# Scan of a bidirectional RWKV layer: TensorE in a written order, products on 64-wide tiles

## The chip, the cores and the metric

The kernel runs on one core of one Trainium2 chip. The metric is device time in microseconds of one execution, measured on the chip. Five engines work side by side, each with its own queue of instructions: TensorE (PE, matrix products into PSUM), VectorE (DVE), ScalarE (ACT), GpSimd (POOL) and SyncE (SP). SP, ACT and POOL also issue DMA transfers between the main memory and SBUF. An engine executes its queue in order and waits where an instruction needs something that another engine or a DMA has not delivered.

## The reference, cut to what matters

One layer works on 128 context tokens and 2048 latent tokens. A combined projection gives r, k, v, gates and a short convolution; eight heads of 64 channels then run a delta-rule recurrence over time, in both directions:

```python
def step(S, inp):
    r_t, w_t, k_t, v_t, kk_t, a_t = inp
    s_kk = jnp.einsum('bdhij,bdhj->bdhi', S, kk_t)
    S = (S * w_t[..., None, :] - s_kk[..., :, None] * (kk_t * a_t)[..., None, :]
         + v_t[..., :, None] * k_t[..., None, :])
    return S, jnp.einsum('bdhij,bdhj->bdhi', S, r_t)
```

Outputs of both directions are added, normalised per head, gated, joined with the convolution's channels and sent through an output projection with a residual and a final norm. Outputs are the new context, the new latent tokens and the final context states. All is float32.

## The kernel before, in words

The program has three parts. `phase1` computes projections, gates and the operands of the recurrence, and stores them in DRAM (`scr_ops`, `scr_vt` and others). `phase2` does the recurrence. `phase3` does the output projection; part of it (`ahead`) is woven into the last stages of the recurrence.

The recurrence is cut into chunks of 64 tokens. Within a chunk the state update is written as products of matrices, with the inverse of a unit triangular matrix of 64 x 64, and only the state passes from chunk to chunk. A **stage** (`NST = 17`) has two groups, one for each direction, with eight chunk units each; a unit has two heads (a head pair `p`). Stage 15 is the context, the others take four blocks of 512 tokens for each of four head pairs. The work of a stage s goes through these parts, in the names of the code and of the profile:

- `partL`: loads the operands of a group into `rr` (issued on SP).
- `partM`: products F and GA (psF, psG, masked by DVE into F and GA), the transposes psQ (copied by ACT into Q), and `blocks`, which puts the two 32 x 32 triangular blocks of GA together (dg, on ACT and DVE) and writes them to DRAM (`scr_at`, issued on ACT).
- `partI`: loads these blocks as `ab` (issued on SP) and inverts all of a stage at once on POOL, by some 50 element-wise instructions of one chain; POOL then writes the result zt to DRAM (`scr_zt`).
- `partW`: loads the stacks `stl` and `str`, the values `sv` and the inverse `zc` (SP), and copies GA and Q into the lower half of the stacks (DVE, ACT).
- `partU`: completes the inverse of 64 x 64 from its blocks of 32: zr is a transposed zc (DVE), psU and psW are products on tiles of 32 x 32, and ACT copies the pieces into `zb`. In the program before, `zb` is a tile of 128 x 128 per unit with zeros outside its two diagonal blocks.
- `partB`: product X (psX, of zb and F), copied with a minus by ACT into the stacks; then product E (psE, of the two stacks), masked by DVE into E.
- `partS`: the scan itself. In eight steps it multiplies E by sv (psS); DVE scales the upper half into the next step's sv (line 998), the lower half goes to the output y.
- `finish`: norm and gate of a finished y, a transpose on TensorE (psT), and the store to `scr_mixT`.

While stage s scans, `partB` runs for stage s + 1, and `partM` and `partI` for stage s + 3 (`LA = 3`, three slots of F, GA and Q). Python generators interleave these parts in the order in which the instructions are written; `ORDER` and the tuple of counts in `main` say which part advances after which scan step. That order is a preference only: a planner reorders each engine's instructions by its own estimate of when operands are ready, and so sets the queues of all engines, SP's included. In the loop, `partI` of stage s + 3 is written at the end of stage s:

```python
            run(m)
            if s + LA + 1 < NST:
                sts[s + LA + 1] = partL(s + LA + 1)
            if s + LA < NST:
                partI(s + LA, sts[s + LA])
```

The load of zc for stage s + 1 is written in the first piece of `partW` (line 891), at the start of stage s; the load of ab is line 847, POOL's first use of it line 856, POOL's output line 868.

PSUM has three pools here: `pm` (two banks: F, GA, Q), `p2` (two banks: X, E, U, W, the transposes of finish) and `pS` (four banks: the scan).

Of the kernel before, what the change touches and what calls it, by code (L numbers as in the profile page):

```python
# [617 lines left out]
NST = 17  # L618
MORD = ("F", "GD", "", "Q")
ON_DVE = "g"  # L620
LA = 3


ORDER_END = ('LbbbL', 'UU', 'U', '', 'BBB', '', '', '', '')
ORDER = ('LbbbL', '', 'U', 'U', 'U', '', 'BBB', '', '')


def phase2(K):
# [42 lines left out]
    def setup_rest():  # L671
# [17 lines left out]
        lt = ring(O.l1, 2, [128, 2, 2, 4, 128], "stl", lambda t_: presetS(vl(t_)))  # L689
        rt = ring(O.l1, 2, [128, 2, 2, 2, 4, 64], "str", presetS)  # L690
        B.lt, B.rt = lambda: vl(lt()), rt
        B.bu = O.l1.tile([128, 16, 32], F32, name="bu")
        B.zb = O.l1.tile([128, 2, 8, 128], F32, name="zb")
        zero(B.zb)
# [30 lines left out]
    def vl(t_):  # L725
        return t_[:].rearrange("p f h u (b t) -> p b f h u t", b=2)

    def presetS(t_):
        for f in range(2):
            for hd in range(2):  # L730
                V.tensor_copy(t_[0:64, 0, f, hd], B.I2[0:64].unsqueeze(1).broadcast_to((64, 4, 64)))
# [34 lines left out]
    def load_stk(t_, g, k, us):  # L766

        units = g.units[us]
        p, c0 = units[0]
        src = S[f"ops{g.d}"][k]  # L770
        n = 4 if p == units[-1][0] else 2
        for i in range(4 // n):
            dst = t_[0:64, 1, us.start // 4, :, n * i:n * (i + 1)]
            x = src[(p + i) * 128:(p + i + 1) * 128, c0 * 64:(c0 + n) * 64]
            if t_ is g.rt:
                D(dst.rearrange("c h u t -> c h (u t)"), x.rearrange("(h c) t -> c h t", h=2))
            else:
                for hd in range(2):
                    D(dst[:, hd], x[hd * 64:hd * 64 + 64].rearrange("c (u t) -> c u t", t=64))
# [6 lines left out]
    def partL(s):  # L786
        st = Ctx()
        st.g = []
        for gi, (d, units, blk) in enumerate(stages[s]):
# [12 lines left out]
        return st  # L802

    def partM(s, st):

        at = S["at"][s]
        for gi, g in enumerate(st.g):
# [3 lines left out]
            g.Q = q[:].rearrange("p (k u) t -> p k (u t)", u=2)  # L811
            def transposes():
                pq = O.pm.tile([128, 4, 128], F32, tag="m", name=f"psQ{s}_{gi}")
                for k in range(4):
                    T.transpose(pq[:, k, :], rr[:, 4, 2 * k:2 * k + 2, :].rearrange("p u t -> p (u t)"), B.idt[:])
                copy("q", g.Q, pq[:])
# [527 lines left out]
```

## Time and profile before

| | us |
|---|---|
| median of 3 runs | 1832.66 (1829.14 to 1839.34) |
| the profiled execution | 1837.07 |
| its span, first to last instruction | 1835.3 |
| scan products (psS), first to last start | 1044.6 to 1669.3 |

In the profile, line numbers are those of the kernel before. PE stands for products on TensorE, PEld for its weight loads, which overlap them. A float32 product is two instructions of each kind. SPq, ACTq and POOLq mark the issue of a DMA. A row of a group of instructions has busy time, mean duration in ns, and the idle time of the engine ahead of it with what ended it. A row of a stretch has its bounds, its length, each engine's busy time with a count of instructions, the granted TensorE clock, the mean busy share of the 16 DMA engines, and GB/s.

### The profile page before, as it was taken

How to read it: one execution, taken by the hardware profiler on the slowest of the kernel's cores; microseconds unless marked ns; L12 is line 12 of the kernel's file. 1: busy time of each engine (PE TensorE's matmuls, PEld its weight loads, DVE VectorE, ACT ScalarE, POOL GpSimd, SP SyncE). 2: the span in 40 equal slices, each digit the busy share in tenths (PEclk: the TensorE clock that was granted, in tenths of full speed). 3: DMA queues.
4: the chain of work that ended last, by engine and by line, in shares of the span. 5: the costliest groups of instructions: out<-in, count | busy, mean ns of one | idle time of the engine just before them, and what ended most of it. 6: DMA issues, size and time to landing. Idle time of an engine off the chain costs nothing. (4 is left out here: it accounts for less than half of the span.)

```text
span 1835.3 us, 35161 instructions
## 1 busy us (share of the span) xinstructions
PE 1685.3 (92%) x13488; PEld 1553.3 (85%) x13488; DVE 1151.2 (63%) x2205; ACT 748.4 (41%) x1471; POOL 595.1 (32%) x1087
## 2 busy tenths in 40 slices
PE   5999899999898999999999798899899899799998
PEld 2998899898888999899899687788798798687886
DVE  5999887446777363588543555576577466656433
ACT  4565545124444131465211353354354336442222
POOL 0132200002221000223055166567657765523221
PEclk9999999999999999999999798799899779899999
DMA  8787787557887353677863665577567655546442
GB/s 350 223 242 240 226 266 266 202 182 161 190 192 189 126 189 132 178 207 201 308 216 120 141 162 116 135 179 176 129 171 165 162 138 143 148 133 210 147 151 98
DMA packets 315384, 335.29 MB, mean 183 GB/s; under 512 B 166920, under 2 KB 263560, under 8 KB 301136
## 3 DMA queue, kind: packets, MB, share of 16 engines
q1 hardware_dynamic: 242912, 323.99, 59.7%
q10 hardware_dynamic: 70944, 4.60, 2.9%
q0 software_dynamic: 1360, 4.46, 0.6%
q8 instruction: 106, 1.74, 0.4%
q14 instruction: 62, 0.51, 0.1%
HBM read 221.16 MB, written 111.82 MB: 181 GB/s over the span
## 5 line engine op out<-in xcount | busy, mean ns | idle before, releaser
L867 POOL TENSOR_TENSOR zt<-zt,ztmp 128x30 f32<-128x30 f32 (+7 forms) x510 | 200.9, 394 | 39.6
L945 PE MATMUL psE<-str,stl 128*128 128x128 f32 x1088 | 158.9, 294 | 22.4 <-DVE E L946 21.4
L945 PEld LDWEIGHTS psE<-str,stl 128*128 128x128 f32 x1088 | 138.9, 201 | 33.4 <-DVE E L946 22.0
L985 PE MATMUL psS<-sv,E 128*128 128x64 f32 x1088 | 159.0, 283 | 8.3 <-DVE sv L998 8.3
L985 PEld LDWEIGHTS psS<-sv,E 128*128 128x128 f32 x1088 | 148.3, 204 | 16.1 <-DVE sv L998 9.8
L864 POOL TENSOR_TENSOR ztmp<-ab,zt 128x60 f32<-128x60 f32 (+7 forms) x255 | 132.2, 518 | 19.9
L946 DVE TENSOR_TENSOR E<-psE,msk 128x512 f32<-128x512 f32 x136 | 93.4, 689 | 59.3 <-PE psE L945 57.6
L314 POOL TENSOR_TENSOR shk<-rawl 128x384 f32<-128x384 f32 (+1 forms) x24 | 20.9, 870 | 274.8 <-ACT rawl L310 274.7
L998 DVE TENSOR_TENSOR sv<-psS,pc 64x128 f32<-64x128 f32 x254 | 67.3, 277 | 60.7 <-PE psS L985 58.6
L934 PE MATMUL psX<-F,zb 128*128 128x128 f32 x544 | 86.2, 307 | 7.6 <-DVE E L946 3.7
L1280 POOL TENSOR_TENSOR z<-z,x 128x512 f32<-128x512 f32 x32 | 43.6, 1366 | 129.1 <-DVE z L1276 107.3
L158 PE MATMUL mmv<-h,w 128*128 128x384 f32 (+1 forms) x192 | 68.0, 354 | 18.7 <-ACT q1r L312 10.6
L934 PEld LDWEIGHTS psX<-F,zb 128*128 128x128 f32 x544 | 74.8, 213 | 12.2 <-ACT zb L713 5.4
L824 PE MATMUL psF<-rr 64*64 64x128 f32 x1088 | 75.1, 300 | 10.3 <-DMA rr<-scr_ops 5.6
L824 PE MATMUL psG<-rr 64*64 64x128 f32 x1088 | 72.0, 295 | 6.9 <-DVE F L826 6.9
L824 PEld LDWEIGHTS psF<-rr 64*64 64x64 f32 x1088 | 52.1, 145 | 21.3 <-issue 4.4
L824 PEld LDWEIGHTS psG<-rr 64*64 64x64 f32 x1088 | 55.7, 143 | 13.7 <-DVE F L826 7.4
L158 PE MATMUL mmg<-h,w 128*128 128x384 f32 (+1 forms) x192 | 63.4, 330 | 3.8 <-ACT ta L374 1.8
L160 PE MATMUL mmv<-h,w 128*128 128x384 f32 (+1 forms) x192 | 66.4, 346 | 0.1
L159 PE MATMUL mmv<-h,w 128*128 128x384 f32 (+1 forms) x192 | 66.2, 345 | 0.0
L195 POOL TENSOR_TENSOR hsls<-sq,hshs 128x384 fp32r<-128x384 f32 (+1 forms) x24 | 30.0, 1252 | 107.9 <-ACT hshs L194 31.7
L158 PE MATMUL mmc<-h,w 128*128 128x384 f32 (+1 forms) x192 | 64.2, 335 | 0.5 <-DMA w<-scr_wsp 0.5
(306 smaller groups left out, 5115.4 us busy)
## 6 DMA issues: line engine op xcount, KB each, us to landing
w<-scr_wsp SPq DMA_DIRECT2D x68, 1024.0 KB, 7.2
scr_wsp<-w SPq DMA_DIRECT2D x34, 1024.0 KB, 5.8
rr<-scr_ops SPq DMA_DIRECT2D x64, 512.0 KB, 5.3
scr_ops<-sp SPq DMA_DIRECT2D x160, 192.0 KB, 4.4
wr<-in_win SPq DMA_DIRECT2D x34, 512.0 KB, 7.4
ab<-scr_at SPq DMA_DIRECT2D x34, 256.0 KB, 4.5
x<-in_x SPq DMA_DIRECT2D x17, 512.0 KB, 3.8
wadas<-in_wada SPq DMA_DIRECT2D x8, 1024.0 KB, 15.0
```

Source lines behind the costliest of these rows:

```text
L158: T.matmul(ps[:, :n], w[:, 0, k], hh[:, 0, k, :n], start=k == 0, stop=False)
L159: T.matmul(ps[:, :n], w[:, 0, k], hh[:, 1, k, :n], start=False, stop=False)
L160: T.matmul(ps[:, :n], w[:, 1, k], hh[:, 0, k, :n], start=False, stop=k == 7)
L824: T.matmul(ps[h][er, a, :].rearrange("p (a b) -> p a b", b=64), w[hr_, u, :], x[hr_, :, u, :], start=True, stop=True)
L864: G.tensor_tensor(tv, ab[:, j:j + 2, j + 2:32].unsqueeze(1).broadcast_to((128, kn, 2, n)), zt[:, :kn, j:j + 2].unsqueeze(3).broadcast_to(( ...
L867: G.tensor_tensor(zt[:, :kn, j + 2:32], zt[:, :kn, j + 2:32], tv[:, :, r], ALU.subtract)
L934: T.matmul(px[:, hd * 2 + a, :], B.zb[:, gi, v, :], g.F[:, v, :], start=True, stop=True)
L945: T.matmul(pe[:, i, hd, :].rearrange("p (b t) -> p b t", b=2), g.lt[:, :, us.start // 4, hd, k + i].rearrange("p b t -> p (b t)"), g.rt[:, ...
L946: V.tensor_tensor(g.E[n][:, k:k + 2].rearrange("p a b c -> p (a b) c"), pe[:].rearrange("p a b c -> p (a b) c"), B.msk[:, ME[g.d]].unsquee ...
L985: T.matmul(sp[gi][:, q, hd, :], g.E[n][:, k, hd, :], sv[:, u, hd, :], start=True, stop=True)
L998: r = V.tensor_tensor(dst, sp[gi][0:64, q], B.pc[0:64, d, 2 * p:2 * p + 2, c:c + 1].broadcast_to((64, 2, 64)), ALU.mult)
L1280: (V if last else G).tensor_tensor(z[:, cs], z[:, cs], xt[:, cs], ALU.add)
```

## The change

TensorE no longer follows the planner in the scan: from stage 0 to the end of stage 13 its instructions run in the order written (`tc.manual_schedule(engines={PE})`). The other engines and SP's queue are still the planner's. `ORDER` has eight slots, one after each scan step; a letter advances one part: b and B the products X and E (b of the stage that is scanning, B of the next), W and U `partW` and `partU` of the next stage, M `partM` of stage s + 3, I `partI` of stage s + 3, l and r the loads of a group of stage s + 4, z the load of the inverse of stage s + 2.

Products E and S, and the transposes of finish, are split into two halves of 64 output rows; X, before one product on a block-diagonal 128 x 128 tile, becomes two of 64 x 64; the transposes Q become products with an identity, on 64 x 64 tiles. X of the second group goes to the pool `pm`. Both stacks have one layout now and are loaded whole, in one transfer per group and operand; the copies from GA and Q are half as many and twice as long. The inverse is loaded straight into `zb`, in eight transfers, two `zb` taking turns; `zc` and the copies from it are gone.

```diff
-MORD = ("F", "GD", "", "Q")
+MORD = ("F", "GD", "Q")
-ORDER_END = ('LbbbL', 'UU', 'U', '', 'BBB', '', '', '', '')
-ORDER = ('LbbbL', '', 'U', 'U', 'U', '', 'BBB', '', '')
+ORDER = ("bM", "bMW", "UUMW", "UMWl", "MBI", "BM", "B", "Brz")
...
+            def tiles(dst, w, x):
                 for a in range(4):
                     for h, hr_ in enumerate((H0, H1)):
                         for e, er in enumerate((H0, H1)):
                             u = 2 * a + e
-                            T.matmul(ps[h][er, a, :].rearrange("p (a b) -> p a b", b=64), w[hr_, u, :], x[hr_, :, u, :], start=True, stop=True)
+                            T.matmul(dst(h, a, er), w[hr_, u, :], x(hr_, u), start=True, stop=True)
...
+            def transposes():
+                ps = banks("Q")
+                tiles(lambda h, a, er: ps[h][er, a, 0:64], rr[:, 4], lambda hr_, u: rr[hr_, 2, u, :])
+                for h in range(2):
+                    copy("q", g.Q[:, h * 4:h * 4 + 4], ps[h][:, :, 0:64])
...
+    def load_z(s, st):
+        st.zb = B.zb()
+        for h in range(2):
+            for sl in range(2):
+                for b in range(2):
+                    r = slice(sl * 64 + b * 32 + h, sl * 64 + b * 32 + 32, 2)
+                    D(st.zb[r, :, b * 32:b * 32 + 32], S["zt"][s][h][:, sl, b].rearrange("u q i -> q u i"))
...
     def partU(s, st):
-        r = V.transpose(st.zr[:].rearrange("p u i -> p (u i)"), st.zc[:].rearrange("p u i -> p (u i)"))
+        r = V.transpose(zr[:], st.zb[:, :, 0:32])
...
-        zf = B.zb[:].rearrange("p d u c -> p (d u) c")
         for r0, r1 in rows:
-            for r in (r0, r1):
-                copy("z", zf[r, :, r], st.zc[r])
-            copy("n", zf[r0, :, r1], pw[r0], True)
+            copy("n", st.zb[r0, :, 32:64], pw[r0], True)
...
     def partB(s, st):
+        for gi, g in enumerate(st.g):
+            pool, tag = (O.pm, "m") if gi and s < NST - 3 else (O.p2, "s")
+            px = [pool.tile([128, 4, 128], F32, tag=tag, name=f"psX{s}_{gi}_{e}") for e in range(2)]
+            for a in range(4):
+                for e, er in enumerate((H0, H1)):
+                    for hd, hr_ in enumerate((H0, H1)):
+                        T.matmul(px[e][hr_, a, :], st.zb[er, gi * 8 + hd * 4 + a, :], g.F[er, hd * 4 + a, :], start=True, stop=True)
+            for e in range(2):
+                for hd, hr_ in enumerate((H0, H1)):
+                    copy("x" if hd else "y", g.fs[64:128, :, hd, e::2], px[e][hr_].rearrange("p a (b t) -> p b a t", b=2), True)
+            yield
...
-                            T.matmul(pe[:, i, hd, :].rearrange("p (b t) -> p b t", b=2), g.lt[:, :, us.start // 4, hd, k + i].rearrange("p b t -> p (b t)"), g.rt[:, :, us.start // 4, hd, k + i], start=True, stop=True)
+                            for b, r in enumerate((H0, H1)):
+                                T.matmul(pe[r, i, hd, :].rearrange("p (b t) -> p b t", b=2), g.lt[:, b, hd, us.start + k + i], g.rt[:, :, hd, us.start + k + i], start=True, stop=True)
...
-                    T.matmul(sp[gi][:, q, hd, :], g.E[n][:, k, hd, :], sv[:, u, hd, :], start=True, stop=True)
+                    for r in (H0, H1):
+                        T.matmul(sp[gi][r, q, hd, :], g.E[n][:, k, hd, r], sv[:, u, hd, :], start=True, stop=True)
...
+        order = tc.manual_schedule(engines={mybir.EngineType.PE})
         for s in range(NST):
+            if s == 0:
+                order.__enter__()
+            if s == NST - 3:
+                order.__exit__(None, None, None)
...
+            for i, _ in enumerate(partS(s, st, nxt)):
                 for f in todo[:1] if s < NST - 3 else todo:
                     next(f, None)
+                next(tail, None)
+                for c in ORDER[i]:
+                    if c in gens:
+                        next(gens[c], None)
+                    elif c in "lr" and s + LA + 1 < NST:
+                        partL(s + LA + 1, ("lr".index(c),))
+                    elif c == "I" and s + LA < NST:
+                        partI(s + LA, sts[s + LA])
+                    elif c == "z" and s + 2 < NST:
+                        load_z(s + 2, sts[s + 2])
```

More of the change, by code (lines that the diff above doesn't have):

```diff
@@ L810, in partM @@
             g.F, g.GA, q = B.slots[s % LA][gi]
[L811 to L816, printed above, removed]
-            def product(dst, w, x, mask, nm):
-                ps = [O.pm.tile([128, 4, 128], F32, tag="m", name=f"ps{nm}{s}_{gi}_{h}") for h in range(2)]
+            g.Q = q[:]
+            def tiles(dst, w, x):
                 for a in range(4):
@@ L948, in partB @@
                 yield
+    ynew = {}
+    sts = {}
+    held = {}
+    pend = []
     def partS(s, st, nxt):
```

146 lines of the change are left out of this document (52 added, 94 removed).

## The prediction

> **What bounds the kernel now.** I read the page first, then stretches of the scan, then the queues between POOL and the loads.
>
> ```profile
> PE 1685.3 (92%) x13488; PEld 1553.3 (85%) x13488; DVE 1151.2 (63%) x2205; ACT 748.4 (41%) x1471; POOL 595.1 (32%) x1087
> PEclk9999999999999999999999798799899779899999
> ```
>
> By the page TensorE is the bound, with a clock that drops only in the scan (slices 23 to 36). The stretches show more. The first row counts the scan's own products (psS, 64 a stage): 896 are 14 stages in 510.90 us, 36.5 a stage.
>
> ```profile
> 1044.70:1555.60 510.90, 132.57 (x896) 0.91 0.62 149
> ```
>
> The next rows are single stretches, with PE, PEld, DVE, ACT and POOL busy, then the granted clock: a stage at full clock, one at 0.78, the last three stages, and the output projection.
>
> ```profile
> 1228.10:1259.00 30.90, 30.90 (x431) 27.82 (x430) 21.60 (x49) 18.58 (x37) 23.49 (x50) 1.00 0.70 168
> 1148.80:1195.60 46.80, 38.18 (x422) 33.67 (x422) 26.37 (x59) 17.27 (x33) 24.96 (x56) 0.78 0.62 151
> 1555.60:1669.40 113.80, 96.90 (x842) 86.97 (x841) 66.97 (x139) 50.63 (x90) 40.86 (x68) 0.91 0.55 160
> 1669.40:1835.30 165.90, 157.25 (x683) 126.97 (x681) 72.74 (x119) 42.30 (x106) 38.44 (x29) 0.99 0.41 143
> ```
>
> TensorE can do a stage in 30.9 us. So what makes the mean 36.5? POOL is busy only 23.5 us a stage, but its inverse starts (dgp) come at exactly that pace: (1557.6 - 1045.9) / 14 = 36.5, and between 1040 and 1600 us POOL waits for its input before 14 of 15.
>
> ```profile
> L856 POOL COPY dgp<-ab x15: 198/204/591, 1045.9 to 1557.6; 128x16 f32<-128x16 f32 x15
>   DMA ab<-scr_at: 129.5, 14
> ```
>
> Why ab is late stands in the timelines of ACT, SP and POOL over one turn:
>
> ```profile
> 1246.09 0.37 ACTq L832 DMA_DIRECT2D scr_at<-dg  x1
> 1244.29 0.36 SPq L801 DMA_DIRECT2D rr<-scr_ops  x1
> 1261.22 1.32 SPq L891 DMA_DIRECT2D zc<-scr_zt  x2
> 1262.64 1.25 SPq L847 DMA_DIRECT2D ab<-scr_at  x2
> 1258.38 0.61 POOL L868 DMA_DIRECT2D scr_zt<-zt  x1 [0.30 <-POOL zt L867]
> 1267.87 0.20 POOL L856 COPY dgp<-ab 128x16 f32<-128x16 f32 x1 [5.88 <-DMA ab<-scr_at]
> ```
>
> The blocks that ab reads were written at 1246. But on SP's queue the load of ab stands behind zc, which waits for zt, which POOL writes out at 1258. So SP stands still for 17 us, and POOL, when it has finished one inverse, waits for its own output to land, for zc to be issued, for ab to be issued and to land: 9.5 us from 1258.38 to 1267.87. With some 26.9 us of work that is a closed loop of 36.4 us. SP's waits and those of the transpose of the inverse (zr) confirm it:
>
> ```profile
> SPq L891 <- DMA scr_zt<-zt: 118.0, 10, 17.0
>   DMA zc<-scr_zt: 31.6, 12
> ```
>
> So the **bound of the scan is POOL's loop through SP's queue**; TensorE's 30.9 us is close behind, and the dropped clock lies largely in time that the loop leaves over.
>
> **The change, part by part.** *Tiles on TensorE.* The paces, from runs of one kind (the last instruction's 0.275 us of latency taken off):
>
> ```profile
> 1336.66 2.00 PE L945 MATMUL psE<-str,stl 128*128 128x128 f32 x16
> 1332.14 1.00 PE L985 MATMUL psS<-sv,E 128*128 128x64 f32 x8
> 1333.80 1.09 PE L824 MATMUL psF<-rr 64*64 64x128 f32 x16
> 1057.85 1.10 PE L824 MATMUL psF<-rr 64*64 64x128 f32 x32
> 34.28 1.07 PE L188 MATMUL psrow<-wadas,scp 128*32 128x512 f32 x8
> ```
>
> E goes at 0.115 us per instruction, S at 0.104 although it streams half as much, F at 0.055 where two tiles run side by side and at 0.027 where four do. Psrow has four 32-wide tiles on all 128 rows: eight instructions of 512 in 1.07 us, where one after the other they would take 8 x 4 x 0.115 = 3.7. So column tiles overlap, also over 128 rows. Weight loads:
>
> ```profile
> L945 PEld LDWEIGHTS psE<-str,stl 128*128 128x128 f32 x1088 | 138.9, 201 | 33.4 <-DVE E L946 22.0
> L824 PEld LDWEIGHTS psF<-rr 64*64 64x64 f32 x1088 | 52.1, 145 | 21.3 <-issue 4.4
> ```
>
> 64 columns fewer save 56 ns, so a load of 128 costs some 0.11: S is bound by its load. Per stage, instructions by pace, two per product: E 64 x 0.115 = 7.4, then 128 in pairs 7.4. S 64 x 0.104 = 6.7, then 128 in pairs: 3.4 if half-wide loads run side by side, 6.7 if one after another; I take 3.4, since S streams half of E. X 32 x 0.115 = 3.7, then 64 in fours, 1.7. F and G 128 between 0.027 and 0.055, 3.5 to 7.0, I take the middle, 5.3, since the trace has both; then 3.5, the written order taking all four tiles in turn. Q 8 x 0.115 = 0.9, then 64 x 0.027 = 1.7 at most. The transposes of finish 0.5, then 0.9. The inverse's U and W, not changed, 2.1. Sum: 26.6 before, 20.7 after.
>
> A change of tile shape costs extra:
>
> ```profile
> 1333.26 0.61 PE L934 MATMUL psX<-F,zb 128*128 128x128 f32 x4
> 1333.80 0.33 PE L824 MATMUL psF<-rr 64*64 64x128 f32 x2
> ```
>
> The last psX starts at 1333.26 + 0.61 - 0.275 = 1333.595, psF 0.205 after it: 0.09 over pace. The slots hold 14 changes a stage (S, E and finish on 128 rows, F, G, Q and X on 64, U and W on 32): 1.3 us, so 22.0. [...]
>
> *The order.* TensorE now executes the slots as written, so a wait stalls all that stands behind it. The nearest rows for what it waits for:
>
> ```profile
> L946 DVE TENSOR_TENSOR E<-psE,msk 128x512 f32<-128x512 f32 x136 | 93.4, 689 | 59.3 <-PE psE L945 57.6
> L998 DVE TENSOR_TENSOR sv<-psS,pc 64x128 f32<-64x128 f32 x254 | 67.3, 277 | 60.7 <-PE psS L985 58.6
> L826 DVE TENSOR_TENSOR GA<-psG,mkg 128x512 f32<-128x512 f32 x68 | 44.8, 680 | 19.4 <-PE psG L824 18.6
> L713 ACT ACTIVATE stl<-psX 64x512 f32<-64x512 f32 x68 | 40.2, 591 | 41.6 <-PE psX L934 40.7
> ```
>
> In slot 5 Q takes the banks of X: four ACT copies of 0.591 for group 0 are still running and four for group 1 follow, 4.7 us against about 2 us of TensorE work (X, S): 2.8 us of stall, then S of slot 6 is late. In slots 0 to 4 DVE has 3 us a slot and more (two scales 0.55, two E masks 1.38, two F or G masks 1.36, the stack copies), against 2.3 to 3.2 of TensorE; with two banks per pool TensorE can run ahead by about a slot. DVE's 21.6 us stay as they are: the stack copies from GA become four of twice the size. I put 3.5 us of lag there (0, if the planner's order on DVE is perfect; 7, the sum of the differences). TensorE's path: 22.0 + 2.8 + 3.5 = 28.3 us a stage at full clock.
>
> *Inverse and loads.* The loads of the inverse go from 2 issues a stage to 8, and are written two stages ahead of use instead of one; stack loads go from 12 to 4. At 0.66 each (zc x2 in 1.32) SP has 1.3 us less in all. Four ACT copies (zb) go, off the path, ACT being 18.6 of 30.9 busy. The load of ab moves from the stage's end to slot 4, and the load of the inverse to slot 7 of the same stage, written three slots after it. If SP's order is that, ab is in place when POOL ends, and the loop is open. What POOL then costs is seen once, where ab came early:
>
> ```profile
> 1346.10 0.20 POOL L856 COPY dgp<-ab 128x16 f32<-128x16 f32 x1 [10.38 <-DMA ab<-scr_at]
> 1372.90 0.61 POOL L868 DMA_DIRECT2D scr_zt<-zt  x1 [0.30 <-POOL zt L867]
> 1375.34 0.52 POOL L852 MEMSET zt<- 128x512 f32 x1 [1.82 <-DMA scr_zt<-zt]
> 1376.26 0.20 POOL L856 COPY dgp<-ab 128x16 f32<-128x16 f32 x1
> ```
>
> 30.2 us from start to start, of which 1.8 is a wait of the next memset on the output: a floor of 28.4 to 30.2. So a stage is the larger of 28.3 and 28.4 to 30.2, and since either engine waits for the other at times, and the clock will still drop now and then, I take 31 (bounds 28.4 and 34).
>
> **The sum.** 14 stages x (36.5 - 31) = 77 us. In the last three stages S and X are cheaper by 3 x 5.3 = 16 us, but other work fills TensorE there in 96.9 of 113.8: I take 8 (0 to 16). Before the scan and after it nothing: phase 1's extra Q is under 2 us. The profiled execution took 1837.07 for a span of 1835.3, and 1837 - 77 - 8 = 1752; the median shown is 4.4 below that execution: **1748**. Its own range: 14 x (36.5 - 28.4) = 113 and 16 give 1704; 14 x 2.5 = 35 and 0 give 1798.
>
> **Rivals.**
>
> *Loop kept, slower.* Only TensorE's order is written; SP's is still the planner's, and the present program writes ab ahead of zc too, yet the queue has zc first in most turns. If the inverse's load is put ahead of ab again, POOL waits for eight issues instead of two: 6 x 0.66 = 4.0 us more a turn, 40.4 us a stage, whatever TensorE saves. 14 x 4.0 = 56 more, 8 less at the end: 1881. It decides wherever a stage's inverse load stands before the ab of the next inverse on SP's queue. For it speaks the present queue, against it that ab is now written a stage's half earlier, and z three slots after it.
>
> *The clock.* At 0.78 the clock was halved for about 44% of 46.8 us, 20.6 us, and the stage took 46.8 - 30.9 = 15.9 more: 0.75 us per us. Over the 14 stages 0.91 means half clock for 18% of 510.9 us, 6.6 a stage, now largely covered by what the loop leaves over. TensorE gets emptier (22 of 31), and slot 5's stall and the slots of U and W are its emptiest. If as much half clock stays and is covered no more, it costs 6.6 x 0.75 = 5.0: 36 a stage, 14 x 0.5 + 8 less, 1818 (1795 to 1845). [...]
>
> *The tiles do not gain.* If 64-wide tiles over 128 rows went one after another, E would cost 14.7 and S 6.7, with the rest 32.6, 36 with the stall: 1815. Psrow speaks against it.
>
> **Chances.** The forecast 0.52; loop kept 0.27; clock 0.15; tiles 0.06. Under 0.5% (9 us) either way is about what cannot be told from no change. Faster: 0.52, 0.09 of the clock's, 0.04 of the tiles', 0.02 of a loop kept in few turns, 0.67. Same: 0.03 + 0.04 + 0.01 = 0.08. Slower: 0.25. The range runs from the forecast's low bound, 1705, to the kept loop, 1885.
>
> **What would show it.** Right: dgp starts 28 to 32 us apart, ab issued on SP before the inverse's load, S pairs at about 0.05 per two instructions, TensorE idle ahead of Q in slot 5, DVE busy over 70% of a stage. Wrong: dgp starts over 36 us apart behind an SP wait on scr_zt (loop kept), granted clock under 0.85 over the 14 stages (clock), or psS runs without a fall of their pace (tiles).

## The result, and the profile after

The change made the kernel slower: 1981.74 us median (1975.15 to 1985.79) against 1836.0 (1829.14 to 1841.8) for the kernel before in the same job, a ratio of 1.0792 with a 95% interval of 1.074 to 1.0843. The forecast was 1748, and the time lies above the whole range. The profiled execution took 1982.16 us, 145 more than that of before (1837.07).

The page of the kernel after, to be read against the page of before: TensorE is busy for a smaller share, and its granted clock stands at 0.7 to 0.8 through the whole scan.

```profile
span 1980.4 us, 42543 instructions
PE 1632.6 (82%) x17364; PEld 1500.2 (76%) x17364; DVE 1132.7 (57%) x2129; ACT 695.5 (35%) x1369; POOL 606.8 (31%) x1088
PEclk7999999999999999999977777777777787879999
```

Stretches of the same kernel (bounds, length, then PE, PEld, DVE, ACT and POOL busy, granted clock, DMA share, GB/s): a part of the scan, the 14 stages, the last three stages, the output projection. The stages are bounded by the scan's products (psS): the first one, the first of stage 14, the last.

```profile
1060.00:1560.00 500.00, 311.34 (x7055) 280.88 (x7053) 231.54 (x487) 152.30 (x283) 264.18 (x573) 0.76 0.50 124
1053.50:1701.00 647.50, 404.76 (x9158) 364.15 (x9154) 307.92 (x643) 197.32 (x365) 345.09 (x744) 0.77 0.50 122
1701.00:1824.90 123.90, 106.91 (x1346) 89.80 (x1346) 74.66 (x146) 45.18 (x81) 42.71 (x65) 0.89 0.49 149
1824.90:1980.40 155.50, 147.65 (x656) 118.50 (x654) 64.23 (x107) 38.59 (x96) 31.98 (x25) 0.99 0.39 136
```

And POOL's starts of an inverse, the view that showed the loop of the kernel before, between 1035 and 1745 us:

```profile
L854 POOL COPY dgp<-ab x15: 200/206/211, 1051.0 to 1694.8; 128x16 f32<-128x16 f32 x15
  DMA ab<-scr_at: 253.8, 15
```

The starts are (1694.8 - 1051.0) / 14 = 46.0 us apart, where before they were 36.5. The scan's products say the same: 14 stages take 647.5 us instead of 510.9, 46.2 a stage and 137 us more in all. The scan also begins 9 us later (1053.5 against 1044.6), the last three stages take 123.9 us instead of 113.8, and the output projection 155.5 instead of 165.9. These four make the 145.

One turn shows what POOL waits for. The timelines of SP, ACT, DVE, POOL and TensorE of the kernel after (start, time, engine, line; in brackets the idle time before and what ended it):

```profile
1354.12 1.90 SPq L874 DMA_DIRECT2D zb<-scr_zt  x3
...
1356.71 3.17 SPq L874 DMA_DIRECT2D zb<-scr_zt  x5
...
1365.37 1.13 SPq L845 DMA_DIRECT2D ab<-scr_at  x2
...
1347.82 0.51 ACT L828 ACTIVATE dg<-GA,hm 128x256 f32<-128x256 f32 x1 [3.44 <-DVE GA L824]
1360.73 0.37 ACTq L830 DMA_DIRECT2D scr_at<-dg  x1
1361.20 2.44 ACT L710 ACTIVATE stl<-psX 64x512 f32<-64x512 f32 x4 [12.87 <-DMA zb<-scr_zt]
1363.66 2.44 ACT L710 ACTIVATE str<-psX 64x512 f32<-64x512 f32 x4
...
1348.36 0.55 DVE L829 SCALAR_TENSOR_TENSOR dg<-GA,hm,dg 128x256 f32<-128x256 f32 x1 [0.58 <-ACT dg L828]
...
1351.73 0.62 POOL L866 DMA_DIRECT2D scr_zt<-zt  x1 [0.30 <-POOL zt L865]
1370.07 0.21 POOL L854 COPY dgp<-ab 128x16 f32<-128x16 f32 x1 [15.05 <-DMA ab<-scr_at]
...
1364.92 0.48 PE L809 MATMUL psQ<-rr 64*64 64x64 f32 x4 [15.76 <-ACT str L710]
```

As before, SP has the loads of the inverse (zb, line 874) ahead of the load of the next blocks (ab, line 845), and they wait for POOL's output at 1351.73. New is ACT's line: its part of the blocks (dg) is done at 1348.3 and DVE's at 1348.9, but ACT issues their transfer scr_at only at 1360.73, after the zb loads. In the compiled program the issue of each scr_at waits on a count, raised when a transfer has landed, which it shares with an earlier transfer. For the second scr_at of a stage, the one shown, that is one of the eight zb loads in 13 of 14 stages, and a store to scr_mixT in the other. ACT's waits ahead of what stands behind this issue show the same numbers (us in total, times, longest):

```profile
ACT stl L710 <- DMA zb<-scr_zt: 104.6, 13, 12.9
ACT stl L710 <- DMA scr_mixT<-yo: 7.9, 1, 7.9
```

So the turn shown has the longest of these waits; the mean is 8.0 us. Behind the issue on ACT's queue stand the copies of X, and behind these TensorE's Q tiles, which leave TensorE idle for 15.8 us. So the blocks of the next inverse are not even written out until the last inverse has been loaded. From POOL's end to its next start pass 1370.07 - 1351.73 = 18.3 us, where before it was 9.5; with some 27 us of POOL's work that is 45.3, near the mean turn of 46.0.

### The profile page after: what moved, and what is told of

It reads as the page before. It is cut to its first block, busy times and chain, and to the rows that moved or that the text cites. A ratio compares the mean times of both kernels' runs of the same rounds, so it can differ in the third digit from the quotient of the medians.

```text
span 1980.4 us, 42543 instructions
## 1 busy us (share of the span) xinstructions
PE 1632.6 (82%) x17364; PEld 1500.2 (76%) x17364; DVE 1132.7 (57%) x2129; ACT 695.5 (35%) x1369; POOL 606.8 (31%) x1088
## 5 line engine op out<-in xcount | busy, mean ns | idle before, releaser
L809 PE MATMUL psQ<-rr 64*64 64x64 f32 x1088 | 45.4, 308 | 152.6 <-ACT str L710 147.6
L938 PE MATMUL psE<-str,stl 128*64 128x128 f32 x2176 | 154.0, 300 | 10.4 <-DVE E L939 8.4
L809 PEld LDWEIGHTS psQ<-rr 64*64 64x64 f32 x1088 | 36.6, 207 | 160.3 <-ACT str L710 153.2
L938 PEld LDWEIGHTS psE<-str,stl 128*64 128x64 f32 x2176 | 138.7, 155 | 14.2 <-DVE E L939 11.5
L984 PE MATMUL psS<-sv,E 128*64 128x64 f32 x2176 | 110.9, 253 | 2.8 <-DVE sv L997 2.2
L984 PEld LDWEIGHTS psS<-sv,E 128*64 128x64 f32 x2176 | 93.7, 162 | 22.0 <-issue 12.5
L710 ACT ACTIVATE stl<-psX 64x512 f32<-64x512 f32 x68 | 40.2, 591 | 117.7 <-DMA zb<-scr_zt 104.6
L809 PE MATMUL psG<-rr 64*64 64x128 f32 x1088 | 54.3, 309 | 31.2 <-DVE F L824 30.9
L905 PE MATMUL psU<-zr,GA 32*32 32x32 f32 x1088 | 31.1, 229 | 54.9 <-DVE zr L897 54.9
L905 PEld LDWEIGHTS psU<-zr,GA 32*32 32x32 f32 x1088 | 28.9, 143 | 57.1 <-issue 56.4
L809 PEld LDWEIGHTS psG<-rr 64*64 64x64 f32 x1088 | 40.8, 151 | 40.2 <-DVE F L824 36.6
```

The lines of the kernel that those rows point to most:

```text
L809: T.matmul(dst(h, a, er), w[hr_, u, :], x(hr_, u), start=True, stop=True)
L905: T.matmul(pu[r1, u, :], st.g[u // 8].GA[r0, u % 8, 96:128], zr[r0, u, :], start=True, stop=True)
L938: T.matmul(pe[r, i, hd, :].rearrange("p (b t) -> p b t", b=2), g.lt[:, b, hd, us.start + k + i], g.rt[:, :, hd, us.start + k + i], start=T ...
L984: T.matmul(sp[gi][r, q, hd, :], g.E[n][:, k, hd, r], sv[:, u, hd, :], start=True, stop=True)
```

## The experiments

Theory L says that this longer loop made the change slow. Rival C says that the written order did, through idle time and the half clock that follows it. The kernel before has medians of 1821.23 to 1836.0 us in the five jobs, so each ratio is to the kernel before in the same job, and a difference in us between two runs is that of their ratios, times 1836.

**The ab loads ahead of the zb loads.** Only the order on SP's queue is tied down; `O.ab` is the last load of ab for the next inverse. In the compiled program this also moves the counts: the second scr_at of a stage now shares its own, in most stages, with a stack load that landed long before. So the edit opens both waits, SP's and ACT's.

```diff
-                    D(st.zb[r, :, b * 32:b * 32 + 32], S["zt"][s][h][:, sl, b].rearrange("u q i -> q u i"))
+                    z = D(st.zb[r, :, b * 32:b * 32 + 32], S["zt"][s][h][:, sl, b].rearrange("u q i -> q u i"))
+                    if s > 1:
+                        tc.add_manual_dep(z.ins, O.ab.name, mybir.DependencyInfo(mybir.DependencyClass.NoSync, mybir.DependencyReason.DATA), reason="order")
```

> The changed kernel, with one thing added: on SP's queue the two ab loads of the next inverse are put ahead of the eight z loads of the inverse before it (nothing else is reordered by hand). Theory L (the inverse's loop through SP and ACT's queue is what made the change slow): each turn of POOL no longer waits for the z loads, so dgp starts come 30 to 34 us apart instead of 46, TensorE no longer idles some 16 us ahead of the Q tiles of slot 5, the granted clock of the scan rises above 0.9, and the time falls to 1740-1800. Rival C (the written order itself, through idle TensorE and the half clock that follows): the same order and the same idle remain, 40 us a stage or more, and the time stays at 1900 or above.

Measured: 1879.14 us, ratio 1.0297 (1.0263 to 1.033). TensorE's written order is the same, and 91 us are gone (1.0792 to 1.0297), so the loop was a large cause. But 1740 to 1800 was missed by 80 us: something else holds a stage at 39 us. The rows of this run: dgp starts 39.3 us apart and what they and SP's load of ab wait for, the same stretch of the scan, and TensorE in one stage.

```profile
L854 POOL COPY dgp<-ab x15: 198/204/207, 1041.3 to 1591.8; 128x16 f32<-128x16 f32 x15
  DMA ab<-scr_at: 153.9, 15
SPq L845 <- DMA scr_at<-dg: 72.4, 14, 8.2
```

```profile
1060.00:1560.00 500.00, 365.97 (x8231) 328.55 (x8230) 275.45 (x578) 176.55 (x329) 301.76 (x666) 0.81 0.60 144
```

```profile
1250.12 1.92 PE L907 MATMUL psU<-zr,GA 32*32 32x32 f32 x64 [3.72 <-DVE zr L899]
...
1260.81 0.43 PE L809 MATMUL psG<-rr 64*64 64x128 f32 x4 [1.61 <-DVE F L824]
...
1268.92 0.33 PE L809 MATMUL psQ<-rr 64*64 64x64 f32 x4 [3.91 <-ACT str L710]
1270.15 1.12 PE L809 MATMUL psQ<-rr 64*64 64x64 f32 x28 [0.90 <-ACT str L710]
```

POOL still waits for ab ahead of every start, but SP now waits for the blocks themselves (scr_at) and no longer for POOL's output: the blocks come late. POOL ended one inverse at 1298.55, and ACT issued the last blocks of the next at 1300.52. TensorE is idle for 134 of 500 us, 10.5 us a turn. The clock of 0.81 costs it at most 84 of its 366 busy us, 6.6 a turn (an estimate: busy time times what the granted clock lacks to 1.0, summed over stretches of 1 us).

**The kernel before with the same edit.** The same dependence, on the two zc loads.

```diff
-                    D(st.zc[h:128:2], S["zt"][s][h].rearrange("u s b q i -> (s b q) u i"))
+                    z = D(st.zc[h:128:2], S["zt"][s][h].rearrange("u s b q i -> (s b q) u i"))
+                    if s > 1:
+                        tc.add_manual_dep(z.ins, O.ab.name, mybir.DependencyInfo(mybir.DependencyClass.NoSync, mybir.DependencyReason.DATA), reason="order")
```

> The kernel before, with the same edit alone: the two ab loads of the next inverse ahead of the two zc loads on SP's queue. My prediction's reading (36.5 us a stage is POOL's loop through SP's queue: 26.9 us of work and 9.5 us from its end to its next start): the loop opens, the next bound is TensorE at 30.9 us a stage with its own waits or POOL's floor of 28.4 to 30.2, so a stage takes 31 to 34 us, dgp starts come that far apart, and 14 stages give 1765-1800. Rival (TensorE bounds the kernel before, and POOL only waits in step with it): 1825-1840, with dgp starts still 36 us apart.

Measured: 1791.82 us, ratio 0.9815 (0.9749 to 0.9882), as expected: dgp starts come 33.7 us apart, and POOL waits for ab before 5 starts instead of 14. The loop through SP's queue did set the pace of the kernel before.

```profile
L856 POOL COPY dgp<-ab x14: 198/204/268, 1068.2 to 1505.9; 128x16 f32<-128x16 f32 x14
  DMA ab<-scr_at: 32.9, 5
```

**No written order.** The region in which TensorE follows the program is taken out of the kernel after.

```diff
-        order = tc.manual_schedule(engines={mybir.EngineType.PE})
...
-                order.__enter__()
...
-                order.__exit__(None, None, None)
```

> The changed kernel without the written order of TensorE: the same slots and pieces are issued, but the planner orders TensorE's queue as it orders the others'. SP still has the z loads ahead of the next ab loads, and the issue of the second scr_at on ACT's queue still waits on the count of a z load. Theory L: the loop is as before this edit, 44 to 47 us a stage, 1940-1990. Rival C (the written order): a stage falls to 36 us or less, 1780-1850.

Measured: 1992.01 us, ratio 1.0913 (1.0878 to 1.0948). The planner's order is no faster while the loop stands: taking the written order out gives none of the 145 us back.

**The two waits apart.** SP keeps zb ahead of ab, but both issues of scr_at are ordered ahead of the zb loads; in the compiled program their counts are then shared, in nearly all stages, with loads that were done long before.

```diff
+                    if 1 < s < NST - 1:
+                        tc.add_manual_dep(z, O.at.name, mybir.DependencyInfo(mybir.DependencyClass.NoSync, mybir.DependencyReason.DATA), reason="order")
+                        for a in O.abs:
+                            tc.add_manual_dep(a, z.name, mybir.DependencyInfo(mybir.DependencyClass.NoSync, mybir.DependencyReason.DATA), reason="order")
```

> The changed kernel with z still ahead of the next ab on SP, but with the two issues of scr_at ordered ahead of the z loads, so that they wait on the count of an earlier stack load and no longer on that of a z load. Theory L, with its two parts: the short loop of the kernel before remains (9.5 us from POOL's end to its next start, plus some 4 us for six more issues, plus 26.9 us of work = 40.4 us a stage), the long way round over ACT's queue is gone: 14 stages at 5.8 us less than 46.2, 1885-1920. If the wait on ACT's queue costs nothing: 1970-1990. If the order of SP's queue costs nothing and that wait is all: 1740-1800.

Measured: 1902.3 us, ratio 1.0432 (1.0386 to 1.0478). POOL's turn in this run:

```profile
1270.18 0.61 POOL L865 DMA_DIRECT2D scr_zt<-zt  x1 [0.30 <-POOL zt L864]
1272.71 5.85 SPq L873 DMA_DIRECT2D zb<-scr_zt  x8
1278.66 1.21 SPq L844 DMA_DIRECT2D ab<-scr_at  x2
1283.72 0.20 POOL L853 COPY dgp<-ab 128x16 f32<-128x16 f32 x1 [10.10 <-DMA ab<-scr_at]
...
L853 POOL COPY dgp<-ab x15: 198/203/208, 1042.6 to 1613.3; 128x16 f32<-128x16 f32 x15
```

From end to start 13.5 us, and (1613.3 - 1042.6) / 14 = 40.8 us a turn, as expected (40.4). So the wait on ACT's queue cost 66 us (1.0792 to 1.0432), and the order on SP's another 25 (to 1.0297). The 25 is what opening SP's queue gives here and no full price of that order, since the next bound, 39.3 us a turn, lies close under 40.8.

**What is left at 39 us a stage.** First the written order again, with the loop open: taken out, and, in another run, Q put ahead of X in the sixth slot.

```diff
-ORDER = ("bM", "bMW", "UUMW", "UMWl", "MBI", "BM", "B", "Brz")
+ORDER = ("bM", "bMW", "UUMW", "UMWl", "MBI", "MB", "B", "Brz")
```

> The changed kernel with the ab loads ahead of the z loads, and without the written order of TensorE. With the written order this took 1879 us, some 40 us a stage, though SP's loop was open; its trace shows TensorE idle 3.7 us ahead of the U tiles, 1.6 ahead of G and 4.8 ahead of Q in one stage. Theory W (those waits, fixed by the written order, are what is left): the planner's order puts other work there, a stage falls to 31-34 us, 1745-1800. Rival T (the tiles and their shape changes, or DVE's and ACT's queues, make the stage long in any order): 1850-1900.

> The changed kernel with the ab loads ahead of the z loads, and one pair of letters exchanged in the written order: in the sixth slot the second half's Q tiles stand ahead of the second half's X tiles. Theory W: the idle time of some 4.8 us ahead of Q, which waits for ACT's copies of the first X, goes; 14 stages by 3 to 5 us, 1810-1840. Rival (the wait only moves: X then waits for ACT's copies of Q, and the copies of X come later): 1865-1890.

Measured: 1869.71 (ratio 1.0249, 1.0205 to 1.0292) without the written order, in the range of rival T, and 1861.05 (1.0198, 1.0154 to 1.0242) with Q ahead. The exchange is worth 18 us, less than its 42 to 70, since X now waits up to 3.5 us for the copies of Q. The planner's order fills TensorE and gains 9 us: it is busy for 431 of 500 us, yet at a clock of 0.79. Its rows, the long stretch, then 4 and 17 us inside it:

```profile
1060.00:1560.00 500.00, 431.45 (x8454) 369.68 (x8452) 279.94 (x593) 180.32 (x336) 309.99 (x680) 0.79 0.62 147
...
1202.00:1206.00 4.00, 2.27 (x64) 2.01 (x64) 3.94 (x9) 1.36 (x4) 3.45 (x8) 0.99 1.05 226
1206.00:1223.00 17.00, 17.00 (x279) 14.75 (x274) 7.05 (x16) 5.18 (x10) 12.09 (x27) 0.50 0.56 153
```

TensorE is busy for 17.00 of 17.00 us and stands at half clock all the time. In those 17 us run F, U, the transposes of finish (T), S, W, G and X, no whole product. Some 2 us ahead of them a wait of 1.73 us for a bank for Q had ended, and the clock was still 0.99. So the fall came behind a wait, and in this row 17 us of TensorE's own small tiles did not bring the clock back from 0.50.

**The S tiles alone, and S and E, in the kernel before** (with ab ahead).

```diff
-                    T.matmul(sp[gi][:, q, hd, :], g.E[n][:, k, hd, :], sv[:, u, hd, :], start=True, stop=True)
+                    for r in (H0, H1):
+                        T.matmul(sp[gi][r, q, hd, :], g.E[n][:, k, hd, r], sv[:, u, hd, :], start=True, stop=True)
```

> The kernel before with the ab loads ahead of the zc loads, and of the tiles only those of S (two products of 64 columns in place of one of 128). Without the S tiles this took 1792 us, 34.3 us a stage, TensorE busy 93% of the span. If TensorE is now what a stage waits for and the S tiles run side by side at 0.03 us an instruction (128 instructions where 64 took 0.107 each: 3.0 us less): 1740-1765. If POOL or the chain of S and its scaling sets the stage now: 1785-1800. If tiles of half the columns cost as much each as whole ones: 1840 or above.

```diff
-                            T.matmul(pe[:, i, hd, :].rearrange("p (b t) -> p b t", b=2), g.lt[:, :, us.start // 4, hd, k + i].rearrange("p b t -> p (b t)"), g.rt[:, :, us.start // 4, hd, k + i], start=True, stop=True)
+                            for b, r in enumerate((H0, H1)):
+                                T.matmul(pe[r, i, hd, :].rearrange("p (b t) -> p b t", b=2), g.lt[:, b, us.start // 4, hd, k + i], g.rt[:, :, us.start // 4, hd, k + i], start=True, stop=True)
```

> As the run with the S tiles alone, and E's products split into halves of 64 columns too. In the changed kernel the E tiles took 0.055 us each where one whole E product took 0.115, so the pairs cost what the whole did: within 8 us of the run with the S tiles alone. If half-wide weights cannot hide here as they do there: slower than that run by 15 us or more.

Measured: 1785.18 (ratio 0.9771, 0.9718 to 0.9823) and 1789.76 (0.9816, 0.9765 to 0.9867), against 0.9815 without tiles. The E tiles cost what whole ones did, as expected, and the S tiles' 3 us a stage buy nothing that can be told from no change.

**A probe of the clock.** Blocks of products without waits, ahead of the scan, in a single run.

```diff
+        whole(260); halves(400, 64); whole(260); halves(230, 128); whole(260)
+        quads(220, 128); whole(260); quads(260, 64); whole(260); small(400); whole(260)
```

> The changed kernel with a stretch of products put ahead of the scan, written one behind the other on TensorE with no waits between them; their results go nowhere. Blocks of 260 whole products (128x128 weights, 128 columns) stand between blocks of smaller tiles: 800 of 128*64 with 64 columns (as S), 460 of 128*64 with 128 columns (as E), 880 of 64*64 with 128 columns (as F, G, X), 1040 of 64*64 with 64 columns (as Q), 800 of 32*32 (as U, W). The question: the planner's version of the changed kernel spent 208 of 500 us at half clock with TensorE busy 86% of the time. Theory H (the granted clock follows how much of TensorE's array works, not whether it works): the clock stays or falls to 0.5 inside blocks of small tiles though they run back to back, first in 64*64 and 32*32, and is 1.0 in the whole blocks. Rival I (only idle time lowers it): 1.0 in all blocks but the first few us. The paces also price the tiles: 0.107 us a whole product, 0.030 for 128*64 with 64 columns, 0.055 with 128, 0.027-0.035 for 64*64, if what the scan showed holds without its neighbours.

The inside of each block, with the columns as above: whole products, 128*64 with 64 columns, 128*64 with 128, 64*64 with 128, 64*64 with 64, 32*32, and whole again.

```profile
1219.00:1275.00 56.00, 56.00 (x504) 56.00 (x503) 0.00 (x0) 0.00 (x0) 0.00 (x0) 1.00 0.00 1
1064.00:1108.00 44.00, 44.00 (x1516) 44.00 (x1512) 0.00 (x0) 0.00 (x0) 0.00 (x0) 1.00 0.02 4
1169.00:1217.00 48.00, 48.00 (x884) 48.00 (x882) 0.00 (x0) 0.00 (x0) 0.00 (x0) 1.00 0.01 2
1278.00:1324.00 46.00, 45.97 (x1674) 45.47 (x1670) 0.00 (x0) 0.00 (x0) 0.00 (x0) 1.00 0.02 5
1385.00:1438.00 53.00, 30.83 (x1895) 28.82 (x1890) 0.00 (x0) 0.00 (x0) 0.00 (x0) 1.00 0.02 4
1505.00:1541.00 36.00, 35.20 (x1284) 34.67 (x1280) 0.00 (x0) 0.00 (x0) 0.00 (x0) 0.50 0.02 5
1546.00:1600.00 54.00, 54.00 (x486) 54.00 (x485) 0.00 (x0) 0.00 (x0) 0.00 (x0) 1.00 0.00 1
```

Of what theory H expects, only the half clock in 32*32 tiles came, here in two positions in turn: busy for 35.2 of 36 us, they ran at 0.50, and in the whole products behind them the clock was 1.00 again. All wider tiles ran at 1.00 here, even 64*64 with 64 columns, by its row busy for only 30.8 of 53 us. The paces are length by count, two instructions to a product: 0.111 us an instruction for whole products, 0.029 and 0.054 for the halves, 0.027 and 0.028 for 64*64. (The expectation's 0.107 is an instruction's, not a product's, price.)

**POOL's restart.** POOL's next memset, which waits for its last output to land, goes behind the first copy of the next inverse, in the kernel before with ab ahead, without and with the S tiles.

```diff
+        if s > 2:
+            tc.add_manual_dep(m0.ins, O.dgp.name, mybir.DependencyInfo(mybir.DependencyClass.NoSync, mybir.DependencyReason.DATA), reason="order")
```

> The kernel before with the ab loads ahead of the zc loads, and POOL's memset of zt (which waits some 3.4 us for the transfer of the last zt out of the buffer that it clears) moved behind POOL's first copy of the next inverse. Without the second edit 1792 us, 34.3 us a stage, and in most stages POOL started again 5 to 6 us after its end. If that restart sets the stage: 2 to 4 us a stage less, 1740-1765. If TensorE (30.9 us a stage and its waits) sets it: 1780-1797.

> The same two edits and the S tiles. Without the memset's move 1785 us: the S tiles took 3.0 us of TensorE's work a stage and gained 7 us in all. If POOL's restart hid that gain: 1725-1755, and at least 15 us under the run without the S tiles. If the clock ate it (72 us at half clock out of 500, 55 without the S tiles): 1770-1790.

Measured: 1784.13 (ratio 0.9782, 0.9731 to 0.9833) and 1784.28 (0.9754, 0.9707 to 0.9801), where the expectations had TensorE with its waits, and the clock. POOL's wait for ab in the run without the S tiles, and the stretch of the scan in the run with them:

```profile
  DMA ab<-scr_at: 102.8, 14
1060.00:1560.00 500.00, 465.84 (x7059) 399.81 (x7056) 341.69 (x735) 254.93 (x475) 340.77 (x768) 0.92 0.64 164
```

With the memset out of the way POOL waits for ab ahead of 14 starts, 102.8 us, instead of 5, 32.9 us: the blocks come no earlier, so POOL's restart is not what holds these at some 33 us a stage. With the S tiles TensorE is busy for 93% of the stretch at a clock of 0.92; it is the likely bound, but why its shorter work in S gains so little was not found. The kernel before with ab ahead, the S tiles and the later memset has the lowest ratio of all runs, 2.5% under the kernel before, but it cannot be told from those with one of these edits less.

**Whole products where TensorE waited.** Into the written order with Q ahead of X, products of the mask with itself go into a part of the scan's bank that is overwritten later.

```diff
+                for k in range((0, 0, 30, 0, 12, 25, 0, 0)[i]):
+                    T.matmul(sp[0][:, 3].rearrange("p h v -> p (h v)"), B.msk[:, 0], B.msk[:, 1], start=True, stop=True)
```

> The changed kernel with the ab loads ahead and Q ahead of X in the sixth slot (1861 us, 86 of 500 us lost to half clock), plus whole products of 128x128 that nobody reads, written into TensorE's order where it waited: 30 ahead of U, 12 ahead of G, 25 ahead of X, 7.2 us of work a stage at 0.107. If the half clock is what is left of the loss: it goes, most stages run at 1.0, and the time falls to 1780-1830 in spite of the added work. If the waits themselves set the stage: 1860-1880 with the higher clock. If TensorE's work sets it: 1900 or above.

Measured: 2008.66, ratio 1.0983 (1.0936 to 1.1031), at a clock of 0.94 in the scan. The size was wrong: 67 products take 15 us, not 7.2, and those ahead of U first waited for a scaling on DVE that reads the same bank. So the run can't say what the half clock costs; it shows that with whole products in the gaps the clock was higher (0.94 against 0.83 in the same order without them), and U's 64 instructions took 1.20 us instead of the 1.92 of the stage shown with ab ahead.

```profile
1249.54 6.96 PE L1007 MATMUL psS<-msk 128*128 128x128 f32 x60 [2.87 <-DVE sv L999]
1256.43 1.20 PE L907 MATMUL psU<-zr,GA 32*32 32x32 f32 x64
```

**Which tiles lower the clock in the scan.** Three runs on the planner's order with ab ahead (1870 us, ratio 1.0249). In the first, U and W have four whole products each in place of 32 tiles of 32*32 (W keeps two tiles), which leaves out their part of the inverse; in the second, S is whole as in the kernel before; in the third, Q is four whole transposes into one bank, with one copy.

```diff
-                T.matmul(pu[r1, u, :], st.g[u // 8].GA[r0, u % 8, 96:128], zr[r0, u, :], start=True, stop=True)
+            T.matmul(pu[:, 4 * a:4 * a + 4, :], B.idt[:], zr[:, 4 * a:4 * a + 4, :], start=True, stop=True)
...
-                tiles(lambda h, a, er: ps[h][er, a, 0:64], rr[:, 4], lambda hr_, u: rr[hr_, 2, u, :])
+                    T.transpose(pq[:, k, :], rr[:, 4, 2 * k:2 * k + 2, :].rearrange("p u t -> p (u t)"), B.idt[:])
```

> The changed kernel with the ab loads ahead and the planner's order of TensorE (1870 us, 104 of 500 us lost to half clock), with the 64 tiles of 32*32 in U and W of a stage replaced by four whole products each against the identity (and two tiles of W kept). It leaves out U's and W's part of the inverse: the off-diagonal blocks are wrong; TensorE's work is 2.0 us instead of 2.4-3.8 a stage, everything that waits for it is the same. Theory H32 (the 32*32 tiles drop the clock, as in the probe): under 50 of 500 us lost to half clock, 1780-1820. Rival (idle time, or too little of the array at work in all of the stage): 80 or more lost, 1845-1870.

> The same kernel (planner's order, ab ahead, 1870 us) with S's products whole again, 32 of 224 ns a stage in place of 64 of 58: 3.4 us of TensorE's work more at full clock. If TensorE's work at the clock of 0.79 sets the stage: 14 times 3.4 to 4 us more, 1915-1930. If whole products bring the clock back by about what they cost: 1855-1885, with under 90 of 500 us lost.

> The same kernel (planner's order, ab ahead, 1870 us) with Q as four whole transposes into one bank and one copy, as the kernel before has it, in place of 16 tiles of 64*64 into two banks and two copies. In the trace of the run with the tiles the half clock begins behind a wait of 1.7 us ahead of Q for a bank that DVE still reads. If that wait starts it: it is gone, under 80 of 500 us lost, 1800-1845. If it makes no difference which window is short of work: 1860-1880.

Measured: U and W whole 1811.62 us, ratio 0.9917 (0.9886 to 0.9947); S whole 1911.44, 1.046 (1.0384 to 1.0535); Q whole 1829.82, 0.9999 (0.9963 to 1.0035). The same stretch in the three runs:

```profile
1060.00:1560.00 500.00, 435.09 (x7568) 364.08 (x7567) 305.67 (x643) 205.31 (x377) 353.71 (x761) 0.91 0.64 162
```

```profile
1060.00:1560.00 500.00, 458.63 (x7019) 393.57 (x7019) 263.80 (x547) 165.39 (x307) 282.95 (x632) 0.78 0.55 135
```

```profile
1060.00:1560.00 500.00, 427.44 (x8362) 356.35 (x8360) 304.93 (x643) 196.15 (x340) 344.96 (x750) 0.85 0.64 159
```

Without the 32*32 tiles the clock goes from 0.79 to 0.91 and 61 us are gone, as expected, at the same busy share of TensorE; at most 1.8 us a stage, 25 us, of that is less work (the expectation's 2.4 to 3.8 against 2.0). The run also puts whole products where the tiles were, so it can't tell which of the two raised the clock; the probe has the tiles alone. With S whole the clock stays where it was (0.78) and the time rises by 39 us, somewhat less than the 48 to 56 expected: here TensorE's work does set the stage, and it was not the S tiles that lowered the clock. With Q whole 46 us are gone and the clock is 0.85, though all 32*32 tiles are there, so they are not the only cause. TensorE's waits ahead of Q are not gone but halved, from 35.0 to 17.9 of 500 us; the run has one bank, one copy and whole products at once, and which of them counts is open.

**The load in place undone.** The kernel after with its written order; the inverse goes into a tile of its own by two transfers, and ACT copies it into zb.

```diff
+            D(st.zc[h:128:2], S["zt"][s][h].rearrange("u s b q i -> (s b q) u i"))
...
+            copy("z", st.zb[r0, :, 0:32], st.zc[r0])
+            copy("z", st.zb[r1, :, 32:64], st.zc[r1])
```

> The changed kernel, written order and all, with one part undone: the inverse comes in by two transfers into a tile of its own and four ACT copies bring it into zb, in place of eight transfers into zb. SP still has z ahead of the next ab, but in the compiled program the issue of scr_at now waits on the count of older loads, no longer on a z load. Theory L: the wait on ACT's queue is gone and the way from POOL's end to its next start is that of the kernel before, 9.5 us, so only the written order and the clock are left: 1870-1905. If the long wait came from something else in the change: 1960-1990.

Measured: 2040.73 us, ratio 1.1175 (1.1107 to 1.1244), far outside the expectation. ACT's timeline, and POOL's end and next start, say why:

```profile
1261.55 2.50 ACT L713 COPY zb<-zc 32x512 f32<-32x512 f32 x4 [12.26 <-DMA zc<-scr_zt]
...
1272.01 0.51 ACT L829 ACTIVATE dg<-GA,hm 128x256 f32<-128x256 f32 x1 [5.16 <-DVE GA L825]
1273.07 0.37 ACTq L831 DMA_DIRECT2D scr_at<-dg  x1
...
1254.38 0.61 POOL L867 DMA_DIRECT2D scr_zt<-zt  x1 [0.30 <-POOL zt L866]
1280.36 0.20 POOL L855 COPY dgp<-ab 128x16 f32<-128x16 f32 x1 [22.71 <-DMA ab<-scr_at]
```

The planner put the copies of the inverse on ACT's queue ahead of the dg of the next blocks. The issue no longer waits on a load of the inverse, but ACT itself waits 12 us for zc and all that follows it is late: the same loop by another road, 26.0 us from POOL's end to its start instead of 18.3. The expectation looked at the counts alone. So fewer transfers do not open the loop: in these runs it is kept where something that waits for one inverse stands ahead of the blocks of the next, on ACT's queue (26.0 us) as on SP's (13.5 with scr_at freed).

## Why the prediction was wrong, point by point

**The bound of the kernel before: right in kind.** POOL's loop through SP's queue did set 36.5 us a stage: opened alone, it gave 33.7 and 1.85% of the time.

**The tiles: right.** By the probe's paces E 128 x 0.054 = 6.9 us, S 128 x 0.029 = 3.7, X 64 x 0.027 = 1.8, F and G 128 x 0.027 = 3.5, Q 64 x 0.028 = 1.8, against forecasts of 7.4, 3.4, 1.7, 3.5 and 1.7. The rival that tiles do not gain is out: whole S products cost 39 us where TensorE sets the stage.

**"The loop is open": the step that failed.** It rested on the order in which the loads are written. SP kept the zb loads ahead of ab, as the kept-loop rival had it, and that rival's price was right as far as it went: 40.4 us a turn forecast, 40.8 measured with scr_at freed. What neither had was the wait on ACT's queue: a transfer that needs nothing from the inverse waited, through a shared count, behind transfers that did, and 46.0 us a turn came of it. Two signs of being wrong came together: dgp starts over 36 us apart, and a clock under 0.85, 0.77 over the 14 stages. The rows that price this step are the two turns above, 18.3 us against 13.5 from POOL's end to its start, and 9.5 before.

**TensorE's path: the second step that failed, by size.** I put 22.0 us of work, 2.8 of waiting ahead of Q and 3.5 of lag, 28.3 a stage at full clock. With ab ahead a turn took 39.3. Of that TensorE idles 10.5 us instead of 6.3: 4.8 ahead of Q, 3.7 ahead of U, 1.6 ahead of G in the stage shown. Some 6.6 go to the clock, and about 22 are left for the work, as forecast. DVE was forecast at over 70% of a stage; after the change it is busy for 231.5 of 500 us, and for 275.5 with ab ahead.

**The clock: named, but at no price of its own in the sum.** The rival gave it 5.0 us a stage and took idle time for the cause, which no run shows by itself. At 0.81, with ab ahead, it is some 6.6 a turn. The rival's 0.75 us per us at half clock was too high: of the 15.9 us by which its stage was longer TensorE was idle for 8.6 and busy for 7.3 more, and only the 7.3 can be the clock's, 0.35 us per us. That the 5.0 still came near is luck: it took 6.6 us of half clock a stage, and 0.81 of 39.3 us means 14.9. Its cause is, as far as the runs show it, in part the 32*32 tiles of U and W, which the change does not touch: alone, in the probe, they ran at 0.50, and with whole products in their place the clock of the scan was 0.91 instead of 0.79. In the kernel before they ran among whole products and the clock was 0.91; after it no whole product is left in the 14 stages and the clock was 0.77, and without the written order, with ab ahead, it was 0.50 for 17 us in which TensorE was busy all the time. In the probe the clock did not go with busy time as the profile shows it: 0.50 at 35.2 of 36 us busy in 32*32 tiles, 1.00 at 30.8 of 53 us in 64*64 tiles.

**The last three stages: wrong in sign.** Forecast 8 us less; measured 10 more, with TensorE busy for 106.9 us instead of 96.9, though S and X were to cost it less there. Forecast as unchanged, the scan's start came 9 us later and the projection took 10 less. No run was made for these.

So of the 234 us between 1748 and 1982, 66 are the wait on ACT's queue, 25 the order on SP's, and 143 are left with the loop open. A turn of 39.3 us instead of 31 makes 14 x 8.3 = 116 of them. The planner's order takes back 9, and on it whole transposes for Q take 46 and whole products for U and W 61 (up to 25 of it work that is left out), each alone; the two were not tried together, and the rest stays open.

## What to carry to other kernels

Follow a loop between engines over every queue on it, the counts that transfers share included: an instruction may stand behind a wait that its own data do not have, as scr_at did here for 8.0 us on average. Order the fetch of the next input ahead of the result's return explicitly; the place in the program says nothing where a planner sets the queues. Where whole products are cut into tiles, look at the granted clock as well as at the paces: here about 22 us of work a stage came as forecast, and with it came a half clock that cost some 6.6 us a turn at most.

## What the runs showed that I had not expected

- The granted clock was low in TensorE's own work: in a row of 32*32 tiles without waits it was 0.50 for 36 us, and after a wait of 1.7 us it was 0.50 for 17 us of mixed small tiles with TensorE busy all the time.
- A 64*64 tile cost 0.028 us an instruction with 64 columns and 0.027 with 128, four tiles in turn: fewer columns saved nothing there.
- A transfer that ACT issues waited for one that SP issues through a shared count, with no data between them: 8.0 us on ACT on average in 13 of 14 stages here, 12.9 at most.
